# Turning the mixers' token-major outputs by transposing DMAs instead of TensorE transposes

## The chip, the cores and the metric

One core of a Trainium2 chip runs the whole program. The metric is device time in microseconds (us); every number below is of one execution or a median of a few.

## The reference, cut to what matters

A decoder trunk of two layers on 512 tokens with 1024 channels. Each layer adds a feed-forward half step, then four token mixers that run side by side on 256 channels each and are joined by one output projection, then a second feed-forward half step.

```python
for l in range(DEPTH):                                   # DEPTH = 2
    x = x + 0.5 * swiglu(rmsnorm(x, ffn1_norm[l]), ...)
    proj = rmsnorm(x, mix_norm[l]) @ w_in[l]
    p_gla, p_lru, p_rw, p_ssd = split_cols(proj, ...)
    ...
    y = jnp.concatenate([y_gla, y_lru, y_rw, y_ssd], axis=-1)
    x = x + y @ w_out[l]
    x = x + 0.5 * swiglu(rmsnorm(x, ffn2_norm[l]), ...)
return rmsnorm(x, final_norm)
```

## The kernel before

All activations stand with channels on the 128 partitions and tokens along the row. A product with weights is made of two-byte halves: a value is split into a float16 head `h` and a bfloat16 rest `lo`, and three matmuls (head by head, head by rest, rest by head) stand for one. The output projection therefore wants its operand as two tiles, `yh` and `yl` (names `y` in the trace), each of 8 channel blocks (`kt`) by 512 tokens: blocks 0 and 1 are GLA, 2 and 3 RG-LRU, 4 and 5 RWKV-7, 6 and 7 Mamba-2 (SSD).

GLA, RWKV and SSD compute their results with tokens on the partitions, in two halves of 256 tokens: a tile `y3` holds two blocks of 128 tokens by 256 channels. `y_from_tokens` turns such a half: for each of two channel blocks TensorE transposes two 128x128 squares into a PSUM bank `yt`, and `put_y` writes the head with ScalarE (`ACT`) and the rest with VectorE (`STT`) from that bank into `yh` and `yl`. It is called six times a layer, twelve times in all: twice for SSD (tile `xD`), twice for RWKV (`yc`), twice for GLA (`sc`). RG-LRU is already channel-major and calls `put_y` itself.

In `mixers`, a loop over six generators (two halves of RWKV, SSD, GLA, RG-LRU and a preparation) writes the program. A host-side clock (`Clock`) estimates when each is ready; where none is, the loop takes a step of `tail`, which first computes the input projection (`pj`, `pt`) and then the output projection (`wo`). The framework's scheduler orders each engine's list afterwards, and at run time each engine takes its list strictly in order. `W_OUT` sets the order of the output projection: its first half adds blocks (6, 7), then (0, 1), which need `y6_*` and `y0_*`; its second half adds (2, 3), then (4, 5), which need both halves of RWKV. There are 8 output blocks of 12 matmuls in each half, 96 matmuls, six of each twelve per group, and three PSUM banks for them. The last half of RWKV (`yc`) is the last result of a layer, and the second half's group (4, 5) waits for it. Results `x` of the residual are fetched back from `x_keep` in DRAM, and each output block is added to them by VectorE.

All plain DMAs are issued by SyncE (SP) in one list, in order, and each waits there for its buffers and data. RWKV's second half passes a small matrix through DRAM and back on that list (`n_scr`, `nb`, `z_scr`, `zt_scr`, `Zt`, `Z`), and the same list carries the weights (`w`, `ra`, `rb`, `rc`), the small tables (`pr_t`, `sm_t`) and `x_keep`. `z` is the first TensorE work on `Zt`, `st` the four-step state recurrence of RWKV, `g` its gate, `go` GLA's output, `P` the first product of the next feed-forward.

Of the kernel before, what the change touches and what calls it, by code (L numbers as in the profile page):

```python
# [11 lines left out]
F16 = mybir.dt.float16  # L12
BF16 = mybir.dt.bfloat16
AF = mybir.ActivationFunctionType
# [28 lines left out]
SY = 2.0 ** -6  # L43
# [125 lines left out]
def kernel(ctx: ExitStack, tc: tile.TileContext, xT, wffn, wmain, wdown, wsmall, pv_d, pr_d, sm_d, cn_d, outT):  # L169
    nc = tc.nc  # L170
# [10 lines left out]
    clk = Clock()  # L181
# [16 lines left out]
    def transpose(out, in_):  # L198
        PE.transpose(out, in_, ident)
        clk.run("PE", 218, (out,), (in_,))  # L200

    def slot(name="s"):
        return sp.tile([128, 512], F32, tag="s", name=name)

    def bank(name="mx"):
        return ps.tile([128, 512], F32, tag="ps", name=name)
# [12 lines left out]
    def STT(out, in0, scalar, in1, op0, op1):  # L219
        V.scalar_tensor_tensor(out=out, in0=in0, scalar=scalar, in1=in1, op0=op0, op1=op1)  # L220
        clk.run("V", 62 + out.free_size() / 0.96, (out,), (in0, in1, scalar))
# [20 lines left out]
    def ACT(out, in_, func, scale=1.0, bias=0.0):  # L242
        A.activation(out=out, in_=in_, func=func, scale=scale, bias=bias)  # L243
        clk.run("A", 190 + out.free_size() * 0.84, (out,), (in_, scale, bias))
# [14 lines left out]
    MUL, ADD, SUB, MIN, MAX = ALU.mult, ALU.add, ALU.subtract, ALU.min, ALU.max  # L259
# [587 lines left out]
    def put_y(kt, src, c0, n, scale=SY):  # L847

        d = yh[:, kt, c0:c0 + n]
        ACT(d, src, AF.Copy, scale=scale)  # L850
        STT(yl[:, kt, c0:c0 + n], src, scale, d, MUL, SUB)

    def y_from_tokens(kt0, y3, t0):

        for i in range(2):
            p = bank("yt")
            for b in range(2):
                transpose(p[:, b * 128:(b + 1) * 128], y3[:, b, i * 128:(i + 1) * 128])
            put_y(kt0 + i, p[:, 0:256], t0, 256)

    def conv4(src, wcol, bcol):

# [213 lines left out]
    def rwkv_half(l, hf, have, out):  # L1076
# [240 lines left out]
        STT(yc, yc, 0.5, pg, MUL, MUL)  # L1317
        yield (yc,)
        y_from_tokens(4, yc2, hf * 256)
        have[f"y4_{hf}"] = True  # L1320


    def ssd(l, have):
# [44 lines left out]
        for c2 in range(2):  # L1368
# [113 lines left out]
            TT(y4, y4, rs.unsqueeze(2).to_broadcast([128, 4, 128]), MUL)  # L1482
            yield (y,)
            y_from_tokens(6, y3, c2 * 256)
            have[f"y6_{c2}"] = True


    def gla(l, have):
# [52 lines left out]
        for c2 in range(2):  # L1541
# [50 lines left out]
            STT(y, y, 0.5, sgt, MUL, MUL)  # L1592
            yield (y,)
            y_from_tokens(0, y.rearrange("p (b f) -> p b f", b=2), c2 * 256)
            have[f"y0_{c2}"] = True

# [306 lines left out]
```

## Time and profile before

| | us |
|---|---|
| median of three runs | 1856.76 (1850.43 to 1856.92) |
| profiled execution, its own time | 1854.53 |
| span of its trace | 1852.8 |
| TensorE (PE) busy | 1815.9, 98% of the span |
| VectorE (DVE) busy | 1378.0, 74% |
| ScalarE (ACT) busy | 978.6, 53% |
| GpSimd (POOL) busy | 73.7, 4% |

The chain that ended last lies on PE for 88% of the span. PE's granted clock is at its full level nearly throughout. The mixers of layer 0 end near 606 us and those of layer 1 near 1519 us. What counts is therefore how long PE is without work, and where.

### The profile page before, as it was taken

What the parts mean: (1) busy time and instruction counts of PE and PEld (TensorE: products, weight loads), DVE (VectorE), ACT (ScalarE), POOL (GpSimd) and SP (SyncE); (2) the same over time, 40 slices, a digit from 0 to 9 for tenths busy, and PEclk for the clock granted to TensorE, in tenths of its full rate; (3) what the DMA queues carried; (4) which work ended last, traced back from release to release, by engine and by line L of the source; (5) the groups of instructions that cost most, each with busy time, mean ns of one, the idle gap of its engine ahead of it and who ended that gap; (6) DMA issues with size and microseconds to landing.
All of it is one profiled execution on the core that took longest, in us unless ns stands there. A gap on an engine that the chain in (4) does not pass through costs nothing.

```text
span 1852.8 us, 33924 instructions
## 1 busy us (share of the span) xinstructions
PE 1815.9 (98%) x14006; PEld 1278.3 (69%) x14006; DVE 1378.0 (74%) x2252; ACT 978.6 (53%) x1578; POOL 73.7 (4%) x75
## 2 busy tenths in 40 slices
PE   7999999999999999999999999999999999999997
PEld 5888844456855888874488886444577558888544
DVE  7988865668768788885589987544877888888633
ACT  7767644432244666664467776434222456666520
POOL 0000000000000000000000000000000000000000
PEclk9999999999999999999999999999999999999999
DMA  8798567522125467637758983733212264674331
GB/s 294 226 273 276 168 219 232 188 72 75 32 83 194 136 185 224 178 124 249 235 161 260 277 243 116 236 138 120 87 39 68 92 200 138 186 222 129 113 107 46
DMA packets 118090, 307.58 MB, mean 166 GB/s; under 512 B 34864, under 2 KB 59440, under 8 KB 103344
## 3 DMA queue, kind: packets, MB, share of 16 engines
q1 hardware_dynamic: 112032, 262.43, 41.1%
q0 software_dynamic: 5904, 42.99, 12.2%
q8 instruction: 109, 1.79, 0.4%
q14 instruction: 45, 0.37, 0.1%
HBM read 272.87 MB, written 32.52 MB: 165 GB/s over the span
## 4 chain that ended last, share of the span: by engine, by line
PE 88%; DVE 6%; ACT 2%; issue 2%; DMA 1%; POOL 0%; SPq 0%; POOLq 0%; DVEq 0%; ACTq 0%
PE d L194 23%; PE B L194 11%; PE A L194 11%; PE pj L194 10%; PE C L194 5%; PE D L194 5%; PE E L194 5%; PE wo L194 3%; PE pt L194 3%; PE P L194 2%; PE z L194 1%; PE go L194 1%; DVE h L216 1%; PE yo L194 1%; DMA w<-in_wdown_dram 1%
## 5 line engine op out<-in xcount | busy, mean ns | idle before, releaser
L194 PEld LDWEIGHTS <-q 128*128 128x128 f16 (+1 forms) x7480 | 734.0, 98 | 104.9 <-ACT q L247 8.0
L194 PEld LDWEIGHTS <-ws 128*128 128x128 f16 (+1 forms) x2706 | 264.4, 98 | 313.6 <-issue 14.9
L194 PE MATMUL d<-h,ws 128*128 128x512 f16 (+3 forms) x2178 | 459.6, 373 | 4.9 <-ACT h L247 3.3
L216 DVE TENSOR_TENSOR q<-ra,q 128x1024 bf16<-128x1024 f32 (+1 forms) x173 | 207.6, 1205 | 42.3 <-ACT q L247 41.9
L194 PE MATMUL B<-xf,q 128*128 128x256 f16 (+2 forms) x1976 | 227.4, 275 | 4.5 <-ACT B L243 4.2
L194 PE MATMUL A<-xf,q 128*128 128x256 f16 (+1 forms) x1968 | 228.9, 273 | 0.0
L247 ACT CAST ws<-w 128x640 f16<-128x640 f32 (+3 forms) x216 | 122.1, 623 | 190.0 <-PE d L194 70.9
L216 DVE TENSOR_TENSOR ws<-w,ws 128x640 bf16<-128x640 f32 (+3 forms) x216 | 141.5, 697 | 86.5 <-ACT ws L247 85.3
L247 ACT CAST q<-ra 128x1024 f16<-128x1024 f32 (+1 forms) x173 | 177.4, 1029 | 29.9 <-DVE ra L216 16.8
L194 PEld LDWEIGHTS <-w 128*128 128x128 f16 (+1 forms) x768 | 73.6, 99 | 86.3 <-issue 9.8
L194 PE MATMUL pj<-xh,w 128*128 128x512 f16 x384 | 122.9, 381 | 0.0
L216 DVE TENSOR_TENSOR q<-rb,q 128x1024 bf16<-128x1024 f32 x88 | 107.3, 1221 | 13.1 <-ACT q L247 13.1
L194 PE MATMUL D<-xf,q 128*128 128x256 f16 (+2 forms) x988 | 115.6, 273 | 0.0
L194 PE MATMUL C<-xf,q 128*128 128x256 f16 (+2 forms) x988 | 115.6, 273 | 0.0
L194 PE MATMUL E<-xf,q 128*128 128x256 f16 (+1 forms) x984 | 114.6, 273 | 0.0
L220 DVE SCALAR_TENSOR_TENSOR dx<-d,R 128x512 f32<-128x512 f32 (+1 forms) x33 | 22.3, 675 | 102.4 <-PE d L194 102.4
L247 ACT CAST q<-rb 128x1024 f16<-128x1024 f32 x88 | 91.5, 1041 | 2.2 <-DMA rb<-in_wffn_dram 2.2
L243 ACT ACTIVATE th<-S 128x512 f32<-128x512 f32 x88 | 55.5, 630 | 58.5 <-DVE S L216 58.4
L216 DVE TENSOR_TENSOR h<-hf,h 128x512 bf16<-128x512 f32 x88 | 57.8, 691 | 26.2 <-ACT h L247 26.0
L216 DVE TENSOR_TENSOR ps<-pw,ps 128x512 bf16<-128x512 f32 x88 | 58.1, 688 | 22.2 <-ACT ps L247 21.9
L194 PE MATMUL pj<-xl,w 128*128 128x512 bf16 x192 | 73.2, 381 | 0.0
L194 PE MATMUL pj<-xh,ws 128*128 128x512 f16 x224 | 69.5, 379 | 0.0
(340 smaller groups left out, 2297.9 us busy)
## 6 DMA issues: line engine op xcount, KB each, us to landing
w<-in_wdown_dram SPq DMA_DIRECT2D x64, 704.0 KB, 4.3
ra<-in_wffn_dram SPq DMA_DIRECT2D x87, 512.0 KB, 7.0
rb<-in_wffn_dram SPq DMA_DIRECT2D x41, 1024.0 KB, 6.6
rb<-in_wffn_dram POOLq DMA_DIRECT2D x41, 1024.0 KB, 9.1
pw<-in_wmain_dram SPq DMA_DIRECT2D x88, 256.0 KB, 5.4
w_scr<-ps SPq DMA_DIRECT2D x88, 256.0 KB, 5.1
w<-w_scr SPq DMA_DIRECT2D x22, 1024.0 KB, 4.8
rc<-in_wffn_dram SPq DMA_DIRECT2D x41, 512.0 KB, 3.8
```

Of the source, the lines that this page charges most:

```text
L194: PE.matmul(out, lhsT, rhs, start=start, stop=stop, skip_group_check=free)
L216: V.tensor_tensor(out=out, in0=in0, in1=in1, op=op)
L220: V.scalar_tensor_tensor(out=out, in0=in0, scalar=scalar, in1=in1, op0=op0, op1=op1)
L243: A.activation(out=out, in_=in_, func=func, scale=scale, bias=bias)
L247: A.copy(out=out, in_=in_)
```

## The change

`y_from_tokens` no longer uses TensorE. The head and the rest are made at once from the token-major half, in one ScalarE and one VectorE instruction of 128x512 each, into a new tile `yq`; then eight transposing DMAs of 128x128 two-byte elements, issued by SP, put the squares into `yh` (four of the head) and `yl` (four of the rest). `clk.dma` tells the host-side clock of them.

```diff
     def y_from_tokens(kt0, y3, t0):
 
-        for i in range(2):
-            p = bank("yt")
-            for b in range(2):
-                transpose(p[:, b * 128:(b + 1) * 128], y3[:, b, i * 128:(i + 1) * 128])
-            put_y(kt0 + i, p[:, 0:256], t0, 256)
+        s = slot("yq")
+        h, lo = (s.bitcast(d)[:, o:o + 512].rearrange("p (b f) -> p b f", b=2) for d, o in ((F16, 0), (BF16, 512)))
+        ACT(h, y3, AF.Copy, scale=SY)
+        STT(lo, y3, SY, h, MUL, SUB)
+        for d, part in ((yh, h), (yl, lo)):
+            for i in range(2):
+                for b in range(2):
+                    nc.sync.dma_start(out=d[:, kt0 + i, t0 + b * 128:t0 + (b + 1) * 128], in_=part[:, b, i * 128:(i + 1) * 128],
+                                      transpose=True)
+                    clk.dma(d[:, kt0 + i, t0 + b * 128:t0 + (b + 1) * 128], part[:, b, i * 128:(i + 1) * 128])
```

SP's list at the end of layer 0's mixers, as a difference (in `y_3847` heads, in `y_3848` rests of RWKV's last half):

```order
 L251 DMA rc<-in_wffn_dram 128x1024 x2
 L251 DMA sm_t<-in_sm_dram 128x1296
 L251 DMA ra<-in_wffn_dram 128x1024 x2
-L251 DMA rb<-in_wffn_dram 128x1024 x2
 L251 DMA pr_t<-in_pr_dram 128x844
+L251 DMA rb<-in_wffn_dram 128x1024
+L862 DMA_TRANSPOSE y_3847<-yq 128x128 x4
+L251 DMA rb<-in_wffn_dram 128x1024
+L862 DMA_TRANSPOSE y_3848<-yq 128x128 x4
 L251 DMA rb<-in_wffn_dram 128x2048
```

One weight load now stands between the four transposing DMAs of the heads and the four of the rests.

SP's list in layer 1 before and at the output projection, as a difference (the three pairs of transposing DMAs in a row are RWKV's first half, then GLA's first and GLA's second half):

```order
 L251 DMA w<-w_scr_14_112 128x2048
-L251 DMA w<-in_wmain_dram 128x2048 x2
+L862 DMA_TRANSPOSE y_13566<-yq 128x128 x4
+L862 DMA_TRANSPOSE y_13567<-yq 128x128 x4
+L251 DMA w<-in_wmain_dram 128x2048
+L862 DMA_TRANSPOSE y_13566<-yq 128x128 x4
+L862 DMA_TRANSPOSE y_13567<-yq 128x128 x4
+L862 DMA_TRANSPOSE y_13566<-yq 128x128 x4
+L862 DMA_TRANSPOSE y_13567<-yq 128x128 x4
+L251 DMA w<-in_wmain_dram 128x2048
 L251 DMA x<-x_keep 128x512 x8
```

The last weight tile of the output projection and the eight `x_keep` loads now stand behind GLA's second half on the list.

PE's list in layer 0 at the end of SSD's first half, as a difference:

```order
 L194 LDWEIGHTS xl
 L194 MATMUL pt<-w,xl 128x256
-L199 MATMUL yt<-cn_t,xD 128x128 x4
 L199 MATMUL bc<-cn_t,cs 128x128 x8
 L194 MATMUL cb<-C_4527,B_4376 128x128
```

The four transposes that needed `xD` are gone, and the transposes of `cs`, which do not need it, follow the projection directly.

## Rows read from the trace of the kernel before

**Rows 1.** The page: busy time, share of the span and instructions of each engine.

```profile
PE 1815.9 (98%) x14006; PEld 1278.3 (69%) x14006; DVE 1378.0 (74%) x2252; ACT 978.6 (53%) x1578; POOL 73.7 (4%) x75
```

**Rows 2.** Waits of PE (who, waited for what: us, times, longest), mixers of layer 0.

```profile
PE yt L199 <- DVE xD L216: 2.8, 2, 1.8
PE st L194 <- DVE PL L216: 1.0, 1, 1.0
...
PE wo L194 <- DVE y L220: 0.7, 1, 0.7
```

**Rows 3.** The tile query for `yt`: min/median/max ns, first and last start.

```profile
L243 ACT ACTIVATE y<-yt x24: 366/378/385, 461.0 to 1499.6; 128x256 f16<-128x256 f32 x24
L220 DVE SCALAR_TENSOR_TENSOR y<-yt,y x24: 404/416/425, 461.5 to 1500.2; 128x256 bf16<-128x256 f32 x24
```

**Rows 4.** The tile query for `y`: RG-LRU's own head and rest.

```profile
L243 ACT ACTIVATE y<-zz x4: 630/630/632, 557.5 to 1478.8; 128x512 f16<-128x512 f32 x4
L220 DVE SCALAR_TENSOR_TENSOR y<-zz,y x4: 682/683/693, 558.2 to 1479.5; 128x512 bf16<-128x512 f32 x4
```

**Rows 5.** PE's timeline at the end of layer 0's mixers (start, length).

```profile
578.02 1.13 PE L194 MATMUL g<-sm_t,sg 32*128 32x256 f32 x4
579.08 7.94 PE L194 MATMUL wo<-y,w 128*128 128x512 f16 x36
586.86 3.40 PE L194 MATMUL wo<-y,ws 128*128 128x512 f16 x15
591.22 0.66 PE L199 MATMUL yt<-cn_t,yc 128*128 128x128 f32 x4 [0.96 <-DVE yc L220]
591.71 1.46 PE L194 MATMUL wo<-y,ws 128*128 128x512 f16 x6
```

**Rows 6.** The same stretch on VectorE: its last step of `yc`.

```profile
590.49 0.68 DVE L220 SCALAR_TENSOR_TENSOR yc<-yc,g 128x512 f32<-128x512 f32 x1
```

**Rows 7.** Tile queries: SP issues (ns); the landings are `Zt`'s, then `pr_t`'s.

```profile
L251 SPq DMA_DIRECT2D Zt<-zt_scr x8: 592/610/638, 440.1 to 1419.8; - x8
DMA to landing us min/median/max: 2.6/2.8/3.2
...
L251 SPq DMA_DIRECT2D w<-in_wmain_dram x2: 332/332/333, 1441.4 to 1467.4; - x2
...
L251 SPq DMA_DIRECT2D nb<-n_scr x4: 592/592/602, 419.1 to 1399.6; - x4
...
DMA to landing us min/median/max: 5.1/5.1/5.1
```

**Rows 8.** The page's DMA issues: KB each, median us to landing.

```profile
x<-x_keep SPq DMA_DIRECT2D x16, 256.0 KB, 6.5
```

**Rows 9.** PE's timeline: GLA's second half in layer 0, and `Zt`'s reader in each layer.

```profile
545.36 0.69 PE L194 MATMUL go<-gv,sc 128*128 128x64 f32 x2
...
556.46 0.66 PE L199 MATMUL yt<-cn_t,sc 128*128 128x128 f32 x4
...
529.59 1.15 PE L194 MATMUL z<-Zt,ms 64*64 64x64 f32 x32
...
1437.06 1.15 PE L194 MATMUL z<-Zt,ms 64*64 64x64 f32 x32
```

**Rows 10.** PE's timeline in layer 1: GLA's second half, two steps of `st`.

```profile
1469.67 0.60 PE L199 MATMUL yt<-cn_t,sc 128*128 128x128 f32 x4
...
1475.40 0.61 PE L194 MATMUL st<-sts,PL 128*128 128x128 f32 x4
...
1476.93 0.61 PE L194 MATMUL st<-sts,PL 128*128 128x128 f32 x4
```

**Rows 11.** SP's timeline in both layers around the moved loads (a row's length spans its issues).

```profile
516.09 1.27 SPq L251 DMA_DIRECT2D Zt<-zt_scr  x2
...
1419.18 1.27 SPq L251 DMA_DIRECT2D Zt<-zt_scr  x2
...
1467.77 5.28 SPq L251 DMA_DIRECT2D x<-x_keep  x8
```

## The prediction

> **What bounds the kernel now.** I read the page's busy times first: PE is busy for 98% of the span and the next engine for 74% [rows 1]. So a cheaper evacuation on ScalarE or VectorE gives nothing by itself, and two things can move the end: work taken off PE, and stretches in which PE finds nothing to do. Next the waits of PE in the mixers, where the change lies: in layer 0 the largest is 2.8 us in two waits of the transposes for SSD's `xD`; then come 1.0 us of `st` and 0.7 us of `wo` for the rests [rows 2]. Last the timelines of PE and SP at the places where a mixer's result is awaited. At the end of layer 0 PE waits 0.96 us for `yc`, transposes, and waits again for the rests [rows 2, 5].
>
> **What is removed.** Four transposes a call. They take PE from 591.22 to the next `wo` at 591.71, 0.49 us [rows 5]; elsewhere the same cadence is a little tighter, and I take 0.46 us, twelve times: -5.5 us. The waits for `xD` stand in front of these transposes, and what follows them in the changed list does not need `xD`; of the 2.8 us I count 2.5 as gained. Together **-8.0 us**. On ScalarE 24 instructions of 378 ns become 12 of 630, on VectorE 24 of 416 become 12 of 683 [rows 3, 4]: -1.5 and -1.8 us on engines that are not the bound, so nothing in the sum.
>
> **What a transposing DMA costs.** No row shows one; 96 are added, eight a call, all on SP's list. Two prices matter: how long each holds the list, and how long after that it lands. The cheapest rows are loads with one run per partition, 0.33 us on the list; those with many short runs (`Zt`, `nb`) take 0.59 to 0.61 us, and `Zt` lands 2.8 us after its start, so 2.2 us after it leaves the list [rows 7]. Below 0.33 us there is no reason to go. The far bound: `w` moves 128 runs and `nb` 1024, so 896 runs more cost 0.26 us; a transpose done element by element has 16,384 moves, which at that rate is 4.7 us more, 5.1 us each. A transpose of two-byte squares is scattered on one side by elements, `Zt` only by 256-byte runs, so I put it above `Zt` but nearer to it than to 5.1: **1.0 us on the list, landing 2.2 us after**, and 0.33 to 1.5 for the range. Where weights are being loaded, landing is longer: 5.1 us for `pr_t` [rows 7].
>
> The Trainium skill bears on this in "VectorE: DVE Perf Modes", section "The three transpose paths": it gives 1309 ns for one 128x128 square through the DMA crossbar and 390 ns on TensorE. Here PE spends 0.49 us on four squares [rows 5], so the page's TensorE price is not what is saved. No row shows its DMA price; by 1.3 us each the sum below would be an estimated +23 us instead of +10.
>
> **End of layer 0.** After `g` (578.02) come 36 matmuls from 579.08 to 586.86, 0.216 us each [rows 5]. By the changed order 54 `wo` can run without RWKV's second half (36 and three banks of six), so PE has work to 579.08 + 54 x 0.216 = 590.8. `yc` is done at 591.2 [rows 6]. Heads: 0.63 on ScalarE [rows 4], four issues of 1.0 us, 2.2 to land: 598.0, so PE idles 7.2 us. Twelve matmuls of heads (2.6 us) bring it to 600.6. The rests are ready by then, but queue on SP behind the heads and one weight load of 0.4: 595.8 + 0.4 + 4.0 + 2.2 = 602.4, plus half of the 2.3 us that a crowded landing adds: 603.6, 3.0 us idle. Before, the idle was 0.96 + 0.65 [rows 2, 5]. Net **+8.6** (+3.0 at 0.33 us, +11.4 at 1.5).
>
> **GLA's second half, layer 0.** It is ready 10.4 us after its last `go` (546.05 to 556.46) [rows 9]. In the changed list the four `st` steps stand ahead of the matmuls that need it, with few `wo` between: steps come 1.53 us apart and take 0.61 [rows 10], so three gaps leave 2.8 us idle that `wo` used to fill, against 1.0 before [rows 2]. PE's work to there I estimate at 16 us. Heads land at 10.4 + 0.6 + 4.0 + 2.2 = 17.2 (1.3 idle), twelve matmuls later rests at 21.2 (1.4 idle). Net **+4.5** (0 to +8.5).
>
> **`x_keep` in layer 1.** The first of these loads was issued at 1467.77 [rows 11]; now it stands behind GLA's second half (ready about 1469.67 [rows 10]): 0.63 + 8.0 + 0.33 later, 1478.6, so 10.9 us late, and it lands 6.5 us after that [rows 8]. The first addition to `x` waits for it, and with it the first of three PSUM banks. Three banks hold 36 matmuls, 7.8 us, which I take as the cover. Net **+3.1** (0 to +7.1). The last weight tile waits with it, but its reader comes some 30 us later.
>
> **End of layer 1.** 84 `wo` stand between `g` and the group that needs RWKV's second half: 1.1 + 18.2 = 19.2 us. With layer 0's 13.15 us from `g` to `yc` [rows 5, 6], heads land at 20.0 and rests at 24.0, 0.8 and 1.4 us late: **+2.2** (0 to +6.2). The weights `ra` for the next product queue behind these eight and come about 8 us later, but they are cast well ahead of it: nothing, and 1 to 3 us if that cover is gone.
>
> **RWKV's trip through DRAM.** In layer 0 the eight of RWKV's first half stand between `z_scr` and `zt_scr`. `Zt`'s second issue (516.7) lands at 519.5 and its reader runs at 529.59 [rows 9, 11], 10 us of cover, about 1.2 less in the changed order: 8.0 us fit in. In layer 1 SSD's second half stands ahead of `z_scr`; the reader (1437.06 [rows 9]) moves some 11 us ahead, which leaves about 4 of the 14 us from 1422.6. SSD's result comes early enough for most of it: **0** at 1.0 us, +3 in layer 0 and +4 in layer 1 at 1.5.
>
> **Sum.** -8.0 + 8.6 + 4.5 + 3.1 + 2.2 = +10.4 us on the profiled 1854.53 us (span 1852.8 and 1.7 around it): 1864.9. The median of the runs is 2.2 us above the profiled one, so **1867 us**.
>
> **Rivals.** *The transposes hold SP's list much longer* (1.5 us or more each; it decides from about 1.2). Then heads and rests trickle in behind each other at all the places above, and `Zt` loses its cover: -8 + 11.4 + 8.5 + 7.1 + 6.2 + 3 + 4 = +32, 1889 us, and more beyond that price. For it: eight in a row, the rests always behind the heads. Against it: no row of this list holds it over 0.7 us. The price that the Trainium skill gives, named above, would fall here. *They are as cheap as `Zt`* (0.61 or less) and not slower than before: the end of layer 0 costs 596.4 - 590.8 + 0.3 - 1.6 = 4.3, GLA's half 1.8, `x_keep` fits under the three banks, and the sum is -1.9: 1855 us; at 0.33 us some -5, 1852 us. It decides at about 0.65 us on the list. For it: `Zt`'s rows, and landings without HBM on either side. *The rearranged lists alone* help or hurt by another 10 us, since the host-side clock now sees different ready times; PE's waits before are only a few us, so there is little to gain.
>
> **How the numbers follow.** Measurements of this kernel (1850.43 to 1856.92) tell a change of over 0.5%, 9.3 us. Forecast (0.65 to 1.2 us a transpose, 1857 to 1876): 0.42, of which 0.17 lies within 0.5% and 0.25 is slower. Expensive transposes: 0.27, all slower. Cheap: 0.25, of which 0.05 is faster by over 0.5% and 0.20 within. Lists alone: 0.06, halved between faster and within. So faster 0.08, same 0.40, slower 0.52. The range 1850 to 1890 leaves out the far part of the expensive case (about 0.12) and some 0.06 below.
>
> **What would show it.** The time of a `DMA_TRANSPOSE` on SP and its landing; PE without `yt`; PE idle ahead of the first `wo` on a `y` at the end of layer 0, around 7 us, then 3; `x` waiting for `x_keep` in layer 1. I am wrong if the idle of PE in the mixers stays near 6 us, if transposes land late by other traffic and not by the list, or if PE waits at a step of RWKV's chain.

## The result and the profile after

The changed kernel is slower: 1897.64 us median of four runs (1896.1 to 1899.55) against 1853.6 us for the kernel before in the same session, a ratio of 1.0245 (95% interval 1.023 to 1.0261). That is 44 us more where 10 were forecast, and outside the range given. The profiled execution took 1898.44 us with a span of 1896.7, 43.9 us above that of before.

The page of the changed kernel, busy time of each engine and the granted clock in 40 slices:

```profile
PE 1822.3 (96%) x13869; PEld 1276.4 (67%) x13958; DVE 1375.1 (72%) x2240; ACT 978.8 (52%) x1566; POOL 73.7 (4%) x75
...
PEclk9999999999988899999999999999999989999999
```

Against [rows 1], PE's time without work grew from 36.9 us (1852.8 - 1815.9) to 74.4 us (1896.7 - 1822.3), by 37.5. And PE is busy 6.4 us longer although 48 transposes, some 5.5 us by the prediction's count, are gone: about 12 us more (an estimate) for the same matmuls, in slices in which the clock row falls from 9 to 8, which are those of the mixers.

What PE waits for, over the whole span of the changed kernel (us, times, longest):

```profile
PE wo L194 <- DMA y<-yq: 18.9, 8, 4.8
PE z L194 <- DMA Zt<-zt_scr: 8.8, 4, 6.8
...
PE st L194 <- DVE sts L220: 3.7, 5, 1.0
PE wo L194 <- DVE x L220: 3.6, 2, 1.9
...
PE ra L194 <- DVE cv L220: 2.1, 1, 2.1
```

None of these stood among the larger waits before; those for `xD` [rows 2] are gone. The first is the transposed operand itself, the second RWKV's trip through DRAM, the fourth VectorE's additions to `x`. The prediction would have put that wait down to the `x_keep` loads; the last experiment shows that they are not the reason.

The transposing DMAs, by the tile query for `yq` (min/median/max ns on SP's list; then landing, from the start of the issue):

```profile
L862 SPq DMA_TRANSPOSE y<-yq x96: 1094/1230/2356, 461.0 to 1538.8; - x96
...
DMA to landing us min/median/max: 2.2/2.3/4.1
```

One holds the list for 1.23 us, twice as long as a `Zt` load [rows 7], and lands 1.1 us after it leaves it. Eight are 10 us. The Trainium skill gives 1309 ns for one square in "VectorE: DVE Perf Modes", section "The three transpose paths"; the time on the list is near it, though the page does not say that they come one after the other.

SP's timeline in layer 0 at RWKV's trip (the second column of a merged row spans all its issues and the waits among them):

```profile
460.98 32.00 SPq L862 DMA_TRANSPOSE y<-yq  x16
493.07 1.29 SPq L251 DMA_DIRECT2D n_scr<-ms  x2
...
517.28 0.57 SPq L251 DMA_DIRECT2D z_scr<-zb  x1
517.95 10.18 SPq L862 DMA_TRANSPOSE y<-yq  x8
528.18 0.59 SPq L251 DMA_DIRECT2D zt_scr<-ztb  x1
530.70 1.27 SPq L251 DMA_DIRECT2D Zt<-zt_scr  x2
```

`Zt` is loaded at 530.70 where it was 516.09 [rows 11], 14.6 us later: the eight between `z_scr` and `zt_scr` are 10.2 of these, and `z_scr` itself was already 4.5 us late (512.79 before). PE's reader of `Zt`, which stood at 529.59 [rows 9], and the end of layer 0:

```profile
533.38 0.44 PE L194 MATMUL z<-Zt,ms 64*64 64x64 f32 x2 [6.79 <-DMA Zt<-zt_scr]
...
616.38 1.44 PE L194 MATMUL wo<-y,ws 128*128 128x512 f16 x3 [3.38 <-DMA y<-yq]
622.21 1.46 PE L194 MATMUL wo<-y,ws 128*128 128x512 bf16 x3 [4.39 <-DMA y<-yq]
624.52 15.84 PE L194 MATMUL wo<-y,ws 128*128 128x512 bf16 x62 [0.85 <-DMA y<-yq]
```

SP's list beside these last rows:

```profile
612.77 4.92 SPq L862 DMA_TRANSPOSE y<-yq  x4
617.74 0.58 SPq L251 DMA_DIRECT2D rb<-in_wffn_dram  x1
618.41 4.92 SPq L862 DMA_TRANSPOSE y<-yq  x4
```

They are read together. The first channel block needs two of the four heads: the second starts at 612.77 + 1.23 = 614.0, lands 2.3 us later, 616.3, and PE goes on at 616.38. The rests begin at 618.41; by the same count their second lands at 621.9 and their fourth at 624.4, and PE goes on at 622.21 and 624.52. Here PE follows SP's list step by step, to within 0.3 us. Three matmuls take 1.44 us in these rows, 0.48 each, where [rows 5] show 0.22. The granted clock there is at the lower of its two levels, 0.50 of full (1.2 of 2.4 GHz), and at the upper one again from 634 us on. Windows of the changed kernel (last three columns: clock, DMA share, GB/s):

```profile
616.38:617.82 1.44, 1.44 (x3) 0.26 (x3) 1.01 (x1) 0.40 (x1) 0.00 (x0) 0.50 0.16 34
634.00:640.00 6.00, 5.95 (x29) 2.70 (x29) 4.65 (x12) 4.71 (x9) 0.00 (x0) 1.00 0.81 257
```

### The profile page after: what moved, and what is told of

Its sections match the earlier page's. It is cut to its first block, busy times and chain, and to the rows that moved or that the text cites. A ratio compares the mean times of both kernels' runs of the same rounds, so it can differ in the third digit from the quotient of the medians.

```text
span 1896.7 us, 33848 instructions
## 1 busy us (share of the span) xinstructions
PE 1822.3 (96%) x13869; PEld 1276.4 (67%) x13958; DVE 1375.1 (72%) x2240; ACT 978.8 (52%) x1566; POOL 73.7 (4%) x75
## 5 line engine op out<-in xcount | busy, mean ns | idle before, releaser
L554 POOL DMA_DIRECT2D rb<-in_wffn_dram x41 | 36.2, 883 | 788.9 <-DMA rb<-in_wffn_dram 387.0
```

The source lines that it names most:

```text
L554: nc.gpsimd.dma_start(out=t, in_=wffn[s, n, :, 3072:5120], accum_op=ADD)
```

## The experiments

Each was timed against the kernel before on the same chip in the same session. Theory 1 says that the transposing DMAs' time on the list is the cause; theory 2 that the order in which the mixer loop deals its steps, changed by what the host-side clock is told, costs the time by itself.

**Only the lists.**

```diff
+        keep = clk.run
+        clk.run = lambda *a, **k: None
         for i in range(2):
             p = bank("yt")
...
             put_y(kt0 + i, p[:, 0:256], t0, 256)
+        clk.run = keep
+        clk.run("A", 190 + 512 * 0.84, (), (y3,))
+        clk.run("V", 62 + 512 / 0.96, (), (y3,))
...
+        clk.eng["DMA"] = t
```

> The instructions of the kernel before (TensorE transposes, no transposing DMA), but the host-side clock is told what the changed kernel tells it, so that the mixer loop deals its steps in the changed kernel's way. If the transposing DMAs themselves cost the 44 us (theory 1), this runs within 8 us of before, 1846 to 1862. If the rearranged lists cost it (theory 2), it is slower than before by most of the 44 us, above 1875.

1857.36 us, ratio 1.0022 (1.0011 to 1.0033): 4 us. Theory 2, as the main cause, falls.

**From ScalarE's list.**

```diff
-                    nc.sync.dma_start(out=d[:, kt0 + i, ...
+                    nc.scalar.dma_start(out=d[:, kt0 + i, ...
```

> The changed kernel with the 96 transposing DMAs issued from ScalarE's list instead of SP's; PE's order stays nearly the same. Theory 1, in the form that SP's list is what is clogged: the wait of z for Zt (7.5 us in layer 0) and that of wo for x go, with the slow clock behind them, so about 1880 to 1887; heads and rests still come 1.2 us apart. The rival form, that any list is held 1.2 us by each and ScalarE's is worse to hold: ScalarE stands still 10 us a call, and the time is 1900 or above. Theory 2 (lists alone) expects no change, 1895 to 1900.

1947.94 us, ratio 1.0518 (1.0495 to 1.0542): 51 us worse than from SP, the rival form. PE's longest waits in this run:

```profile
PE wo L194 <- DMA y<-yq: 23.1, 7, 7.0
PE gs L194 <- ACT qm L243: 14.9, 3, 8.7
PE ra L194 <- DVE cv L220: 11.2, 2, 7.6
```

The DMA holds ScalarE's list as long as SP's (median 1252 ns), and there computing waits behind it: PE waits for ScalarE's `qm`, which it never did to speak of before. The wait for `Zt` did go, as theory 1 had it: PE waits for it nowhere in this run. SP was the better of the two places.

**RWKV's trip on GpSimd's list, and its control.** Both kernels get the same edit, at all five places of the trip; the second is the kernel before.

```diff
-        dma(out=bass.AP(zts, 0, blocks), in_=ztb)
+        dma(out=bass.AP(zts, 0, blocks), in_=ztb, eng=nc.gpsimd)
```

> The changed kernel with RWKV's trip through DRAM (n_scr, nb, z_scr, zt_scr, Zt, Z) issued from GpSimd's list, so that it no longer stands behind transposing DMAs; all else as changed. Theory 1: the wait of z for Zt in layer 0 (7.5 us) and layer 1 (1.3 us) goes, and the slow clock after it (about 3 us), so 1884 to 1890. Theory 2: no change, 1893 to 1902.

> The kernel before (no transposing DMA) with RWKV's trip through DRAM on GpSimd's list: the control for the run in which that move was made on the changed kernel and won 14 us. If it won there because the trip left its place behind the transposing DMAs, it wins nothing here, 1849 to 1861; if the move is worth 14 us by itself, about 1839.

The changed kernel with the trip moved takes 1883.04 us, ratio 1.0172 (1.0153 to 1.0192): 30 us over before in its session, where the changed kernel was 44 over. The kernel before with the same move takes 1853.29 us, ratio 1.0004 (0.9992 to 1.0017): the move is worth nothing by itself. (GpSimd's list carries plain DMAs in the kernel before too, 41 of the `rb` weight loads.) So about 14 of the 44 us are the trip standing behind transposing DMAs. PE's reader of `Zt` in layer 0 runs without a wait again, in the run with the trip moved:

```profile
525.97 1.15 PE L194 MATMUL z<-Zt,ms 64*64 64x64 f32 x32
```

**Twice as many, and twice as many of half the size.** The first repeats every transposing DMA; the expectation on record speaks of the rests alone and of 144, but the loop holds the heads too, so 192 ran. The second cuts each into two of 64 tokens.

```diff
                 for b in range(2):
-                    nc.sync.dma_start(out=d[:, kt0 + i, ...], in_=part[:, b, ...], transpose=True)
+                    for _ in range(2):
+                        nc.sync.dma_start(out=d[:, kt0 + i, ...], in_=part[:, b, ...], transpose=True)
```

```diff
+                    for q in range(2):
+                        nc.sync.dma_start(out=d[:, kt0 + i, t0 + b * 128 + q * 64:t0 + b * 128 + (q + 1) * 64],
+                                          in_=part[q * 64:(q + 1) * 64, b, i * 128:(i + 1) * 128], transpose=True)
```

> The changed kernel with the 48 transposing DMAs of the rests issued twice (the second writes the same values), so 144 in all. Theory 1: 4.9 us more on SP's list at each of the twelve calls; where a result is awaited (end of both layers, GLA's second half, x_keep, Zt) that is 5 us more each, plus the slower clock, so 20 to 35 us more, 1918 to 1932. If the transposes' time on the list is not what counts, less than 8 us more.

> The changed kernel with each transposing DMA cut in two of 64 tokens, 192 in all with the same bytes. If the list is held for a time by bytes, 0.6 us each, there is no change, 1893 to 1902; if it is held for a fixed time per DMA, 1.2 us each, the time is that of the run with 192 whole ones, about 1985.

1987.42 us (ratio 1.0733, 1.0712 to 1.0755) and 1985.28 us (1.0725, 1.0709 to 1.0741). The same time to a tenth of a per cent, with twice the bytes in one as in the other. The rows of the doubled and of the halved kernel:

```profile
L863 SPq DMA_TRANSPOSE y<-yq x192: 1095/1230/2359, 461.7 to 1629.4; - x192
```

```profile
L863 SPq DMA_TRANSPOSE y<-yq x192: 1089/1226/2374, 462.6 to 1626.5; - x192
```

At these two sizes the list is held for a time per DMA and not by its bytes. The second 96 cost 90 us, 0.94 us each, three quarters of the time that each holds the list.

**One mixer at a time.** `y_from_tokens` is kept in both forms, and one mixer's four calls take the DMAs.

```diff
+        (y_by_dma if kt0 == 6 else y_by_pe)(kt0, y3, t0)
```

> Transposing DMAs for SSD's four calls alone (32 of them); RWKV and GLA by TensorE as before. Nothing waits long for SSD's result, but RWKV's n_scr (layer 0) and z_scr (layer 1) stand behind it on SP's list. Theory 1 (the list): 1.8 us less PE work, the wait for xD gone, and up to 5 to 10 us lost where the trip is late in layer 1; 1852 to 1864. The reading that every transposing DMA costs its share of the 44 us wherever it stands (0.46 us each): 1868.

> Transposing DMAs for GLA's four calls alone (32). Theory 1: GLA's second half is awaited in layer 0 (4 us and a slower clock after it), and x_keep stands behind it in layer 1 (3.6 us): 1858 to 1870. Equal shares: 1868, so this run alone does not tell them apart; with the other two it does.

> Transposing DMAs for RWKV's four calls alone (32): the last result of each layer, awaited with nothing behind it, and in layer 0 the first half between z_scr and zt_scr. Theory 1: the dearest of the three, Zt 7 us, both ends 7 us each, and the slow clock, 1870 to 1885. Equal shares: 1868.

SSD alone 1858.36 us (ratio 1.0031, 1.0013 to 1.0048), GLA alone 1879.94 (1.0154, 1.0139 to 1.0169), RWKV alone 1886.25 (1.0188, 1.0168 to 1.0207): 6, 28 and 34 us more than before in that session. Equal shares fall, since the number is 32 in each. But GLA and RWKV alone came out above what theory 1 had expected, and the three add up to 69 us, not 44. The likely reasons, not tested one by one: lateness that falls into a stretch which already waits costs nothing more, and each kernel has its own lists (RWKV alone shows one wait of 18.8 us for `y`, which no other run has). What one call costs cannot be read from such a run.

**SSD's calls, with the trip out of their way.** The two edits above together.

> Transposing DMAs for SSD's four calls alone, and RWKV's trip on GpSimd's list, so that nothing awaited stands behind them. If the 6.5 us that SSD's calls alone cost came from the trip standing behind them, this is level with before or 2 to 4 us under it, 1848 to 1855; if not, 1858.

1853.35 us, ratio 1.0016 (1.0004 to 1.0028). The 6 us become 1 by the medians and 3 by the ratio (0.7 to 5.2): near level, as the first case expected, not under before.

**The slow clock.** 24 matmuls without use follow RWKV's second half, so that PE works through the wait.

```diff
+        if kt0 == 4 and t0:
+            p = bank("fill")
+            f = s.bitcast(F16)[:, 0:512]
+            for n in range(24):
+                mm(p, f[:, 0:128], f, free=True)
```

> The changed kernel with 24 matmuls of no use (head of yq by itself into a spare PSUM bank; 5.2 us at full clock) after RWKV's second half in each layer; their place in PE's list is in the wait for the transposed result. If PE's slow clock behind these waits is caused by the waits, the output projection's second half then runs at 0.22 us a matmul instead of 0.25 to 0.48, about 8 us come back and the time is 1886 to 1893, in spite of 10.4 us more work. If the clock has another cause, the matmuls only fill idle time or add to it: 1896 to 1905.

1899.35 us, ratio 1.0262 (1.0247 to 1.0277): nothing came back. In the changed kernel at the end of layer 1, the wait and what follows:

```profile
1538.71 1.46 PE L194 MATMUL wo<-y,ws 128*128 128x512 bf16 x3 [4.76 <-DMA y<-yq]
1541.22 21.54 PE L194 MATMUL wo<-y,ws 128*128 128x512 bf16 x84 [1.04 <-DMA y<-yq]
```

The same stretch with the matmuls added:

```profile
1529.81 5.35 PE L194 MATMUL fill<-yq 128*128 128x512 f16 x24
...
1540.95 5.79 PE L194 MATMUL wo<-y,ws 128*128 128x512 bf16 x26 [1.47 <-DMA y<-yq]
1548.46 5.35 PE L194 MATMUL wo<-y,ws 128*128 128x512 f16 x24 [1.73 <-DVE x L220]
1554.38 7.93 PE L194 MATMUL wo<-y,ws 128*128 128x512 f16 x36 [0.57 <-DVE x L220]
```

The clock did stay up: 5.79 us for 26 matmuls, 0.22 each, where 84 took 21.54, 0.26 each. The windows from 1540 to 1560, of the changed kernel and of this one (last columns: clock, DMA share, GB/s), say the same:

```profile
1540.00:1560.00 20.00, 18.85 (x73) 7.97 (x75) 13.94 (x25) 11.05 (x20) 0.93 (x1) 0.83 0.71 243
```

```profile
1540.00:1560.00 20.00, 16.75 (x77) 7.45 (x78) 12.05 (x19) 9.11 (x16) 0.93 (x1) 1.00 0.71 218
```

So the low clock at this place goes with the wait. But here PE then waits for VectorE's additions to `x`, which the slow PE had hidden, and the next product starts at the same time (1562.15 against 1562.59). In layer 0 the added matmuls took the place of some useful ones that the changed list had in front of the wait, PE still waited 3.8 us behind them for the rests, and its clock was at 0.50 again (623.4 to 628.0). My expectation had left out that VectorE is next.

**Awaited results or all of them.** The trip stays on GpSimd's list; the first kernel uses DMAs for the eight calls that nothing waits for, the second for the four others, the second halves of GLA and RWKV.

```diff
+        (y_by_dma if not (kt0 in (0, 4) and t0) else y_by_pe)(kt0, y3, t0)
```

```diff
+        (y_by_dma if (kt0 in (0, 4) and t0) else y_by_pe)(kt0, y3, t0)
```

> Transposing DMAs for the eight calls whose result is not awaited (SSD's two halves, the first halves of GLA and RWKV; 64 of the 96), TensorE transposes for the four awaited ones (the second halves), and RWKV's trip on GpSimd's list. If what is left of the 44 us after the trip (30 us) is the lateness of awaited results, these 64 cost nothing: 1849 to 1857, at best 3 us under before for 3.7 us less PE work. If each transposing DMA costs its share wherever it stands, 1868 to 1875.

> The complement: transposing DMAs for the four awaited second halves alone (32 of the 96), TensorE transposes for the rest, RWKV's trip on GpSimd's list. Lateness of awaited results: most of the 30 us, 1873 to 1885. Equal shares: 1862.

The first, with 64 transposing DMAs, takes 1849.48 us, ratio 0.998 (0.9966 to 0.9994), 1 to 6 us under before. The second, with 32, takes 1891.13 us, ratio 1.0208 (1.0182 to 1.0233), 39 us over, more than the 30 that were expected. PE's waits in the first (the longest that the kernel before has not), then in the second:

```profile
PE z L194 <- DMA Zt<-zt_scr: 2.2, 1, 2.2
```

```profile
PE wo L194 <- DMA y<-yq: 28.3, 11, 4.6
```

The second kernel's PE at its two awaited places in layer 0:

```profile
563.99 0.61 PE L194 MATMUL wo<-y,w 128*128 128x512 f16 x1 [2.04 <-DMA y<-yq]
569.07 1.46 PE L194 MATMUL wo<-y,w 128*128 128x512 bf16 x3 [3.63 <-DMA y<-yq]
571.70 1.04 PE L194 MATMUL wo<-y,w 128*128 128x512 bf16 x2 [1.16 <-DMA y<-yq]
...
604.37 1.01 PE L194 MATMUL wo<-y,ws 128*128 128x512 f16 x2 [4.57 <-DMA y<-yq]
609.38 1.46 PE L194 MATMUL wo<-y,ws 128*128 128x512 bf16 x3 [3.99 <-DMA y<-yq]
612.00 18.66 PE L194 MATMUL wo<-y,ws 128*128 128x512 bf16 x72 [1.17 <-DMA y<-yq]
```

In layer 0 each awaited call has the same three waits: first heads, first rests, last rests. In layer 1 PE waits for the rests of both (4.28 and 1.09 us, 4.33 and 1.29) and 0.78 us for heads once. So the 30 us arise at the four awaited calls. The two kernels do not quite add up: 39 over and 3 under make 36, where all 96 with the trip moved are 30 over.

**`x_keep` too.** As the first move, with one load more.

```diff
-                                dma(out=x[n], in_=x_keep[:, n, :])
+                                dma(out=x[n], in_=x_keep[:, n, :], eng=nc.gpsimd)
```

> The changed kernel with RWKV's trip and the x_keep loads both on GpSimd's list. The run with the trip alone there took 1883 us; if x waiting behind GLA's second half costs what PE's waits for VectorE's x show (3.6 us), 1878 to 1881; if it is covered by the late transposes themselves, 1881 to 1885.

1885.33 us, ratio 1.0175 (1.0149 to 1.02), level with the run that moved the trip alone (1.0172). The loads did go out earlier, from 1477.94 us instead of 1488.96, and PE still waits 3.6 us for VectorE's `x`. The loads' place on SP's list costs nothing that this can tell. The changed kernel's trace shows what that wait is instead:

```profile
1523.59 0.69 DVE L216 TENSOR_TENSOR yc<-yc,rs 128x512 f32<-128x512 f32 x1 [1.53 <-POOL rs L256]
1524.20 0.69 DVE L220 SCALAR_TENSOR_TENSOR x<-wo,x 128x512 f32<-128x512 f32 x1
```

```profile
1524.94 2.75 PE L194 MATMUL wo<-y,w 128*128 128x512 f16 x11 [1.65 <-DVE x L220]
```

The addition to `x` stands on VectorE's list behind a step of RWKV's last half (`yc`), which waits for GpSimd. The first addition of this layer (1509.01) had waited for no load. The kernel of "Only the lists", without any transposing DMA, has a wait of 2.2 us for VectorE's `x` in the same stretch of layer 1.

## Why the prediction was wrong

The direction was the likelier one given and most of the places were the right ones, but the sum was short by 34 us. The step that failed first is RWKV's trip, put at 0; the second is that PE's matmuls run slower behind each wait, which no term held.

*What is removed, -8.0 us*: the transposes went and so did the waits for `xD`. For the eight calls of the kernel with 64 transposing DMAs the term would give an estimated 6.2 us (eight times 0.46, and 2.5); that kernel is 1 to 6 us faster, so at best the term is right in size.

*What a transposing DMA costs*: put at 1.0 us on the list and 2.2 to land; measured 1.23 and 1.1. The errors offset each other for the first result of a call and add for what queues behind. That it is so by the DMA and not by its size was not considered. The price alone does not explain the miss: between the prediction's own +10 at 1.0 us and +32 at 1.5, 1.23 us gives an estimated +20.

*RWKV's trip, 0 us*: it took each group of eight alone against 10 us of cover. In layer 0 the trip passes two groups, and they add: `n_scr`, behind SSD's sixteen, was left out of the sum and left 3.9 us late (493.07 against 489.18), `z_scr` 4.5, and `zt_scr` stood behind 10.2 more, 14.6 for `Zt` in all. PE waited 7.5 us for it in layer 0 and 1.3 in layer 1; with what follows, moving the trip gave 14 us back. Of the expensive rival's +3 and +4, the first was short and the second too much. "PE waits at a step of RWKV's chain" was one of the prediction's own signs of being wrong.

*End of layer 0, +8.6*: PE's three waits there are 3.4 + 4.4 + 0.85 = 8.6 us, less 1.6 before, +7.0. The reason given, the rests behind the heads and a weight load, is the right one, but that the size is near is partly luck. For the heads 7.2 us were forecast and 3.4 measured, mainly since PE goes on when two of the four heads have landed, 1.1 us after the list; for the rests 3.0 and 5.2, since only three matmuls stood between and not twelve. (The +11.4 for 1.5 us leaves out the half of a crowded landing that the +8.6 counts; with it the same sum gives 12.6.)

*GLA's second half in layer 0, +4.5*: `st` waits 3.7 us in five gaps, 1.0 before, and `wo` 3.95 us for the rests of `y`; about 6.6, under-sized.

```profile
584.29 1.44 PE L194 MATMUL wo<-y,w 128*128 128x512 bf16 x3 [2.97 <-DMA y<-yq]
586.71 9.71 PE L194 MATMUL wo<-y,w 128*128 128x512 bf16 x33 [0.98 <-DMA y<-yq]
```

*End of layer 1, +2.2*: 4.8 + 1.0 = 5.8 us, under-sized, near the 6.2 given for 1.5 us a DMA.

*`x_keep`, +3.1*: nothing. No addition to `x` waits for a load in the changed kernel, and the 3.6 us that PE waits for `x` have another cause. (With the trip moved VectorE waits 1.6 us for one load, and PE's 3.6 us are the same.)

*Not in the sum at all*: behind the waits PE's matmuls run at 0.26 to 0.48 us instead of 0.22, some 12 us of busy time. With the trip moved, the profiled span is 27.6 us longer than before: PE is 23.7 us longer without work (60.6 against 36.9) and 3.9 us longer busy, in spite of the transposes that are gone. What the slow matmuls cost by themselves stays open: at the one place where the clock was held up, the end of layer 1, VectorE was next and nothing was won. That the 30 us belong to the four awaited calls is shown by the two complements.

The rival of expensive transposes, said to decide from about 1.2 us, is what happened; its 1889 us were short for the same two reasons, the trip in layer 0 and the slow matmuls.

## What to carry to other kernels

Replacing engine work by DMAs moves it to the issuing list: price the list first (time per DMA, how many, what stands behind them), and add up every group that a dependent chain passes, not each alone against its cover. Replace only what turns a result that nobody awaits: with the trip on another list, 64 of these 96 are free or a little better than free, and the 32 awaited ones alone cost 39 us, more than all 96 did there (30). The version with 64 and the trip on another list is the fastest measured here, 0.2% under before.

## What the runs showed of the hardware

A transposing DMA of two-byte elements between tiles of on-chip memory held the issuing list 1.23 us for 128x128 and 1.226 us for 64 tokens by 128 channels, on SP; 1.25 us for 128x128 on ScalarE, where it held up computing too. GpSimd's list took RWKV's `Zt` loads at 0.69 us each instead of 0.61, at no cost in time. PE's granted clock was at 0.50 behind waits of 3.4, 4.4 and 6.8 us in layer 0 of the changed kernel, and at 1.00 at the end of layer 1 when 24 added matmuls had filled most of the wait there, yet nothing was won.
